# Gate/up and down of a SwiGLU layer by seven block products instead of eight

## The chip, the cores and the metric

One core of one Trainium2 chip runs the whole program, a hybrid decoder layer in float32. The metric is device time in microseconds (us), the median of several runs. The engines are TensorE (matmuls and transposes; PE in the rows, its weight loads PEld), VectorE (DVE), ScalarE (ACT), GpSimd (POOL) and SyncE (SP, which here only issues DMAs).

## What the kernel computes

The layer has a token-mixing part (four parallel mixers, gated and merged, then an output projection) and a channel-mixing part, SwiGLU. The change is in the second:

```python
h2 = rmsnorm(x, norm2_g)                      # x: 1024 tokens x 1024 features
g_ff, up_ff = jnp.split(h2 @ w_gate_up, 2, axis=-1)   # 2816 columns each
return x + (jax.nn.silu(g_ff) * up_ff) @ w_down       # then a last rmsnorm
```

## The kernel before

Every operand of a large product is held as hi + lo, two float32r values that sum to the float32 one (`split`, L126 to L128: ScalarE casts hi, VectorE subtracts to get lo), and a product is three matmuls into the same PSUM bank (`mm3`, L119 to L124). A matmul has a 128x128 stationary operand and a moving one of 128x512. Weights come from DRAM in pieces of 128 x 1024 (512 KB) by SP's queue and are split when they land (`load_w`, L111).

The 1024 tokens are two halves of 512 (HT). Tokens of half 0 are normalised and transposed while the merge of half 1 runs (the list `later`, L688 and L738); those of half 1 are written to DRAM (`x2d`), read back and normalised inside the first four blocks of gate/up (`norm2`, L747): ScalarE squares, VectorE scales the rows, TensorE turns eight pieces of 128 into two PSUM banks, `split` takes them out. The result `h2[half]` holds features on partitions, 8 pieces of 128 features by 512 tokens.

Gate/up: for each half, for each of NF = 22 blocks of 128 hidden columns, `group` (L174) makes the gate product and the up product, 8 pieces x 3 matmuls each. ScalarE takes Silu of the gate, VectorE multiplies by up, and the result is split into `ff`, which stays in SBUF (11 tiles, each two blocks). Down: `tok_out` (L647), for each half and each 512 output columns, runs over 11 pairs of hidden blocks and 4 token tiles, with `ff` as the stationary operand and the split weight as the moving one, into four PSUM banks; `evict_f` (L797) adds the residual, sums the squares for the last norm, and `store_f` scales and stores. So each half's weights of gate/up and down are loaded and split again, 88 and 44 pieces.

The order on each engine is made by the framework's scheduler: it simulates the program by a table of costs and issues what is ready, the earlier traced first; tiles of a pool tag share a fixed number of buffers, and an instruction that needs a buffer waits for its last readers. Each engine then runs its queue strictly in that order, SP's DMA issues and GpSimd's too. `in_order` (L130) fixes what is traced inside it to the traced order. PSUM has eight banks of 128x512 float32: two "mm", three "z", two "tr", one "o".

Of the kernel before, what the change touches and what calls it, by code (L numbers as in the profile page):

```python
# [46 lines left out]
def tile_hybrid_trunk(  # L47
# [19 lines left out]
    wp = ctx.enter_context(tc.tile_pool(name="wp", bufs=2))  # L67
    hp = ctx.enter_context(tc.tile_pool(name="hp", bufs=2))
    sp = ctx.enter_context(tc.tile_pool(name="sp", bufs=4))
    ps = ctx.enter_context(tc.tile_pool(name="ps", bufs=1, space=bass.MemoryType.PSUM))  # L70
# [59 lines left out]
    @contextmanager  # L130
    def in_order():
        """Keeps TensorE, ScalarE and VectorE to the order traced."""
        names = [(nc.tensor, "matmul"), (nc.tensor, "transpose"), (nc.scalar, "copy"), (nc.scalar, "activation"),
                 (nc.vector, "tensor_sub"), (nc.vector, "tensor_add"), (nc.vector, "tensor_mul"),
                 (nc.vector, "scalar_tensor_tensor"), (nc.vector, "tensor_scalar")]
# [44 lines left out]
    x2d = [dp.tile([P, D], F32, name=f"x2d{t}") for t in range(8)]  # L180

    # =============================== token mixers ===============================
# [3 lines left out]
    class Fill:  # L186
        """Projection work that is traced in between the steps of a mixer, to keep TensorE fed."""
# [140 lines left out]
    def scores(st, j, c, mask):  # L328
        """Units of at most 512 keys of the raw scores of query tile c, masked on its own block."""
# [43 lines left out]
    def attend(st, p, rows, br, per_step):  # L373
# [11 lines left out]
        def turned(pq, s0):  # L385
            """The weights of two key tiles, key-major, hi and lo."""
# [259 lines left out]
    # =============================== merge and output projection ===============================  # L646
    def tok_out(nkp, act, src, evict, last=False):  # L647
        """Token-major product of feature-major activations with a weight, 512 columns at a time."""
        for ch in range(2):
            acc = [psum("z", f"acc{i}") for i in range(3)] + [psum("o", "acc3")]  # L650
            todo = [(kp, t) for kp in range(nkp) for t in range(4)]
            if last and ch:
                # the token tiles end one after the other
                k0, k1 = nkp - 2, nkp - 1
                todo[-8:] = [(k0, 0), (k0, 1), (k1, 0), (k1, 1), (k0, 2), (k1, 2), (k0, 3), (k1, 3)]
# [10 lines left out]
            with in_order() if last and ch else nullcontext():  # L666
                for t in range(4):
                    evict(t, ch, acc[t])
# [5 lines left out]
    for half in range(2):  # L674
# [57 lines left out]
        def evict_o(t, ch, acc, half=half, x2=x2, hh=hh):  # L732
            c = slice(ch * 512, (ch + 1) * 512)
            nc.vector.tensor_add(x2[t][:, c], acc, x2[t][:, c])
            if ch == 1:
                nc.sync.dma_start(x2d[4 * half + t], x2[t])
                if half == 0:
                    later.append(lambda: norm_T(x2[t], gp.tile([P, D], F32, tag="yr", name="xn2", bufs=1),  # L738
                                                g2, hh, t * P))
# [5 lines left out]
    fp = ctx.enter_context(tc.tile_pool(name="fp", bufs=2, reuse_waits="tile"))  # L745

    def norm2(t):  # L747
        r = fp.tile([P, D], F32, tag="xr", name="x2r", bufs=4)
        nc.sync.dma_start(r, x2d[4 + t])
        norm_T(r, fp.tile([P, D], F32, tag="xr", name="xn2", bufs=4), g2, h2[1], t * P)  # L750

    for half in range(2):
        ff = []
        for f in range(NF):
            wg = load_w(wgu[2 * f])
            og = psum("mm", "mmf")
            group(og, wg, h2[half])
            wu = load_w(wgu[2 * f + 1])
            ou = psum("mm", "mmf")
            group(ou, wu, h2[half])  # L760
            sl = fp.tile([P, HT], F32, name="sl", bufs=2)
            nc.scalar.activation(sl, og, AF.Silu)
            nc.vector.tensor_mul(sl, ou, sl)  # L763
            if f % 2 == 0:
                ff.append(fp.tile([P, 2, 2, HT], F32R, tag="ff", name="fft", bufs=11))
            split(ff[-1][:, f % 2, 0, :], ff[-1][:, f % 2, 1, :], sl)
            if half == 0 and f == 0:
                g2 = load_g(fp, norm2_g, "gf", 1)
            if half == 0 and f < 4:
                norm2(f)  # L770
            if later:
                later.pop(0)()

        xr, ssf = [], []
        for t in range(4):
            r = fp.tile([P, D], F32, tag="xr", name="xr", bufs=4)
            nc.sync.dma_start(r, x2d[4 * half + t])
            xr.append(r)
            ssf.append(sp.tile([P, 2], F32, tag="ssf", name="ssf"))
        if half == 0:  # L780
            gf = load_g(fp, final_g, "gf", 1)
        lo_, hi_ = slice(0, 512), slice(512, 1024)

        def rstd_f(t, ssf=ssf):
# [94 lines left out]
```

## Time and profile before

| | |
|---|---|
| median of 3 runs | 1767.07 us (1766.25 to 1767.4) |
| profiled execution, span from first to last instruction | 1765.0 us (its own time outside the span is not listed) |
| TensorE busy | 1737.9 us, 98% |
| VectorE busy | 817.4 us, 46% |
| ScalarE busy | 606.8 us, 34% |
| DMA | 171.22 MB, 97 GB/s on average |

Busy time is the union of an engine's instructions; matmuls overlap, so the mean of one is longer than the distance from one start to the next. A group's line gives line number, engine, operation, output and inputs, shape, count, then busy time and mean, then the engine's idle time just before and what released it.

### The profile page before, as it was taken

To read this page: it belongs to the slowest core of one execution; us is meant where nothing else is said; L and a number is where in the kernel's file an instruction comes from. 1 tells how busy PE (TensorE), PEld (TensorE's weight loads), DVE (VectorE), ACT (ScalarE), POOL (GpSimd) and SP (SyncE) were. 2 spreads that over 40 slices of the span, in tenths; PEclk is the share of its full clock that TensorE was granted. 3 is DMA by queue.
4 is the path that set the end of the run, shared out by engine and by line. 5 is a ranking of instruction groups with operands and counts; after the bars stand their busy time and mean duration, and the time that the engine had idled before them with its cause. 6 is when DMAs were issued, how large, how long until landed. Compare 5 with 4: busy or idle time off the path is not lost.

```text
span 1765.0 us, 19954 instructions
## 1 busy us (share of the span) xinstructions
PE 1737.9 (98%) x7973; PEld 1396.9 (79%) x7973; DVE 817.4 (46%) x1168; ACT 606.8 (34%) x975; POOL 47.3 (3%) x108
## 2 busy tenths in 40 slices
PE   7999999999999999999999999999999999999998
PEld 7778777777788888888888888888888888888886
DVE  5676667787733435443434453333323333333232
ACT  5433455655432222243222242222212322222222
POOL 1011000010000000000000000000000000000000
PEclk9999999999999999999999999999999999999999
DMA  4311111101152223343223363222222522222222
GB/s 174 108 54 51 51 32 32 31 20 32 33 166 95 96 96 126 109 163 115 96 96 105 128 233 119 96 93 92 92 96 95 191 94 96 96 96 96 96 95 96
DMA packets 52620, 171.22 MB, mean 97 GB/s; under 512 B 6160, under 2 KB 9264, under 8 KB 52528
## 3 DMA queue, kind: packets, MB, share of 16 engines
q1 hardware_dynamic: 51952, 167.85, 28.3%
q10 hardware_dynamic: 576, 2.10, 0.4%
q8 instruction: 63, 1.03, 0.2%
q14 instruction: 29, 0.24, 0.0%
HBM read 156.27 MB, written 13.65 MB: 96 GB/s over the span
## 4 chain that ended last, share of the span: by engine, by line
PE 89%; DVE 4%; issue 1%; ACT 1%; POOL 0%; POOLq 0%; DVEq 0%; ACTq 0%
PE mmf L124 9%; PE mmf L123 9%; PE mmf L122 9%; PE mmg L124 7%; PE mmg L123 7%; PE mmg L122 7%; PE acc L124 6%; PE acc L122 6%; PE acc L123 6%; PE mm L122 3%; PE mm L124 3%; PE mm L123 3%; PE o L399 2%; PE pr L123 2%; PE pr L122 2%; PE pr L124 2%
## 5 line engine op out<-in xcount | busy, mean ns | idle before, releaser
L128 DVE TENSOR_TENSOR wlo<-wraw,whi 128x1024 fp32r<-128x1024 f32 x250 | 306.0, 1224 | 602.3 <-ACT whi L127 595.7
L127 ACT CAST whi<-wraw 128x1024 fp32r<-128x1024 f32 x250 | 262.1, 1048 | 865.4 <-PE mmf L123 317.7
L124 PE MATMUL mmf<-g0h,wlo 128*128 128x512 f32 x352 | 139.2, 396 | 0.0
L124 PE MATMUL mmf<-g1h,wlo 128*128 128x512 f32 x352 | 139.2, 395 | 0.0
L123 PE MATMUL mmf<-g1l,whi 128*128 128x512 f32 x352 | 138.7, 394 | 0.0
L123 PE MATMUL mmf<-g0l,whi 128*128 128x512 f32 x352 | 138.7, 394 | 0.0
L122 PE MATMUL mmf<-g0h,whi 128*128 128x512 f32 x352 | 138.5, 393 | 0.0
L124 PE MATMUL acc<-whi,fft 128*128 128x512 f32 x352 | 138.4, 393 | 0.0
L122 PE MATMUL acc<-whi,fft 128*128 128x512 f32 x352 | 138.3, 393 | 0.0
L122 PE MATMUL mmf<-g1h,whi 128*128 128x512 f32 x352 | 138.2, 393 | 0.0
L123 PE MATMUL acc<-wlo,fft 128*128 128x512 f32 x352 | 137.4, 390 | 0.0
L124 PE MATMUL mmg<-h1h,wlo 128*128 128x512 f32 x256 | 101.4, 396 | 0.1
L124 PE MATMUL mmg<-h0h,wlo 128*128 128x512 f32 x256 | 101.3, 396 | 0.0
L123 PE MATMUL mmg<-h0l,whi 128*128 128x512 f32 x256 | 100.9, 394 | 0.0
L123 PE MATMUL mmg<-h1l,whi 128*128 128x512 f32 x256 | 100.8, 394 | 0.0
L122 PE MATMUL mmg<-h1h,whi 128*128 128x512 f32 x256 | 100.8, 394 | 0.0
L122 PE MATMUL mmg<-h0h,whi 128*128 128x512 f32 x256 | 100.4, 392 | 0.0
L763 DVE TENSOR_TENSOR sl<-mmf,sl 128x512 f32<-128x512 f32 x44 | 30.4, 691 | 150.1 <-PE mmf L124 150.1
L122 PEld LDWEIGHTS mmf<-g1h,whi 128*128 128x128 f32 x352 | 66.6, 189 | 15.3
L122 PEld LDWEIGHTS mmf<-g0h,whi 128*128 128x128 f32 x352 | 66.6, 189 | 15.1
L123 PEld LDWEIGHTS mmf<-g1l,whi 128*128 128x128 f32 x352 | 66.1, 188 | 15.5
L123 PEld LDWEIGHTS mmf<-g0l,whi 128*128 128x128 f32 x352 | 66.1, 188 | 15.3
(245 smaller groups left out, 3187.3 us busy)
## 6 DMA issues: line engine op xcount, KB each, us to landing
wraw<-in_wgu_dram SPq DMA_DIRECT2D x88, 512.0 KB, 3.2
wraw<-in_wgate_dram SPq DMA_DIRECT2D x64, 512.0 KB, 3.2
wraw<-in_wd_dram SPq DMA_DIRECT2D x44, 512.0 KB, 3.3
wraw<-in_wmix_dram SPq DMA_DIRECT2D x22, 512.0 KB, 3.3
wraw<-in_wbr_dram SPq DMA_DIRECT2D x16, 512.0 KB, 3.2
wraw<-in_wo_dram SPq DMA_DIRECT2D x16, 512.0 KB, 3.3
xt<-in_x_dram SPq DMA_DIRECT2D x8, 512.0 KB, 9.5
yr<-ydr SPq DMA_DIRECT2D x8, 512.0 KB, 4.4
```

The lines of the kernel that those rows point to most:

```text
L122: nc.tensor.matmul(o, ah, bh, start=start, stop=False)
L123: nc.tensor.matmul(o, ah, bl, start=False, stop=False)
L124: nc.tensor.matmul(o, al, bh, start=False, stop=stop)
L127: nc.scalar.copy(hi, v)
L128: nc.vector.tensor_sub(lo, v, hi.bitcast(F32))
L399: nc.tensor.matmul(o, vv[:, s0 + s, j, :], pt[:, i, s * 256:(s + 1) * 256], start=s0 + s + i == 0, stop=s0 + s + i == ns)
L763: nc.vector.tensor_mul(sl, ou, sl)
```

## The change

The products of gate/up and of down are seen as 2x2 blocks and made by Strassen's scheme in Winograd's form: 7 block products instead of 8, with sums of blocks ahead of and behind them.

Gate/up. The left factor's blocks are gate and up weights (rows) by features 0 to 511 and 512 to 1023 (columns), for one hidden block g of 128 at a time: a11, a12, a21, a22. The right factor's blocks are the two feature halves by the two token halves. `four` makes the four sums of one factor in VectorE, the second from the first and the fourth from the second: of the weights in `blocks_w`, of the tokens in `norm2`, there still token-major, from the normalised tokens of half 0 (kept in DRAM, `xnd`, by a new DMA in `norm_T`) and of half 1. Each token tile of half 1 then has five pieces of 512 features to turn and split: h22, t1 to t4, for 2 tr banks. A product (`prod`) has 4 pieces x 3 matmuls into one of six banks. Products 1 and 2 need tokens of half 0 alone: for g = 0 to 9 they run first (`early`), with the norm of half 1 traced between them and TensorE kept to the traced order, and product 1 and the Silu of gate half 0 go to DRAM (`stash`). Then `rest` runs for g = 0 to 21: the products left, their sums out of PSUM by VectorE, Silu, multiplies.

Down. After each second block, `down_a` makes the four sums of two result blocks and stores all seven left operands in DRAM (`ffd`), and `down_b` loads the down weights, makes their four sums and stores them (`wdd`); both by GpSimd's queue. Then a second stage makes seven products one after the other (`product`), each over 11 hidden pairs and 4 token tiles into four of eight banks; each of its operands (128x512, 256 KB) is loaded from DRAM and split (`operand`). The sums out of PSUM are made by VectorE and, from SBUF, by GpSimd (16 adds of 128x512); the residual, the norm and the stores follow as output blocks become complete, the last product's four token tiles one after the other.

SBUF pools are closed and opened anew: the weight pool and the PSUM pool end after the output projection; gate/up has its own (t2 to t4; ten tiles "x4" of 128x1024 for raw weights, sums, stash, results and norm; six "x2" tiles; four split weight pairs and a fifth of half the size), and down has its own where h2, t2 to t4 and x4 were. The mixers and the layout of the inputs stay as they were.

```diff
-    def norm_T(xt, xn, g, h, c0):
+    def norm_T(xt, xn, g, h, c0, keep):
         ss = norm_stat(xt, xn)
         nc.vector.scalar_tensor_tensor(xn, xt, ss, g, op0=ALU.mult, op1=ALU.mult)
+        nc.gpsimd.dma_start(keep, xn)
         norm_turn(xn, h, c0)
...
+    pq = pqs.enter_context(tc.tile_pool(name="pq", bufs=1, space=bass.MemoryType.PSUM, reuse_waits="tile"))
+    fp = p3.enter_context(tc.tile_pool(name="fp", bufs=2, reuse_waits="tile"))
+    EARLY = 10
...
+    h11 = [v[:, 0:4] for v in h2[0]]
+    h21 = [v[:, 4:8] for v in h2[0]]
+    h22 = [v[:, 0:4] for v in h2[1]]
+    t1 = [v[:, 4:8] for v in h2[1]]
+    t2, t3, t4 = ([fp.tile([P, 4, HT], F32R, name=f"t{i}{v}", bufs=1) for v in "hl"] for i in (2, 3, 4))
+    stash = [dp.tile([P, D], F32, name=f"stash{g}") for g in range(EARLY)]
+    ffd = [dp.tile([P, 7, HT], F32, name=f"ffd{j}") for j in range(NF // 2)]
+    wdd = [dp.tile([P, 7, HT], F32, name=f"wdd{j}") for j in range(NF // 2)]
+    def tile4(name):
+        return fp.tile([P, 1024], F32, tag="x4", name=name, bufs=10)
...
+    def four(s, x11, x12, x21, x22, first):
+        if first:
+            tt(s[0], x21, x22, op=add)
+            tt(s[1], s[0], x11, op=sub)
+            tt(s[2], x11, x21, op=sub)
+            tt(s[3], x12, s[1], op=sub)
...
     def norm2(t):
...
+        s = halves(tile4("tok")) + halves(tile4("tok"))
+        four(s, a0, b0, a1, b1, False)
+        yield
+        for v, to in zip([b1] + s, (h22, t1, t2, t3, t4)):
+            tr = pq.tile([P, 512], F32, tag="tr", name="trn", bufs=2).rearrange("p (k t) -> p k t", k=4)
+            for k in range(4):
+                nc.tensor.transpose(tr[:, k, :], v[:, k * P:(k + 1) * P], identf)
+            split(to[0][:, :, c], to[1][:, :, c], tr)
+    def prod(w, h):
+        o = pq.tile([P, HT], F32, tag="pp", name="pp", bufs=6)
+        for k in range(4):
+            c = slice(k * P, (k + 1) * P)
+            mm3(o, (w[0][:, c], w[1][:, c]), (h[0][:, k, :], h[1][:, k, :]), k == 0, k == 3)
+        return o
+    def early(g):
+        w = split2(load_raw(2 * g))
+        st = tile4("st")
+        nc.scalar.copy(st[:, :512], prod(half_of(w, 0), h11))
+        tt(st[:, 512:], prod(half_of(w, 1), h21), st[:, :512], op=add)
+        nc.scalar.activation(st[:, 512:], st[:, 512:], AF.Silu)
+        nc.gpsimd.dma_start(stash[g], st)
+    def blocks_w(g):
+        r0, r1 = load_raw(2 * g), load_raw(2 * g + 1)
+        a11, a12, a21, a22 = r0[:, :512], r0[:, 512:], r1[:, :512], r1[:, 512:]
+        s23, s14 = tile4("s23"), tile4("s14")
...
+        four(s, a11, a12, a21, a22, True)
...
+    def rest(g, w):
+        if g < EARLY:
+            st = tile4("st")
+            nc.sync.dma_start(st, stash[g])
+            p1, sl = st[:, :512], st[:, 512:]
+        else:
+            p1, sl = tile2("p1"), tile2("sl")
+            nc.scalar.copy(p1, prod(w[1], h11))
+            tt(sl, prod(w[2], h21), p1, op=add)
+            nc.scalar.activation(sl, sl, AF.Silu)
+        u2, u3 = tile2("u2"), tile2("u3")
+        tt(u2, prod(w[6], t2), p1, op=add)
+        tt(u3, prod(w[7], t3), u2, op=add)
+        p5 = prod(w[5], t1)
+        tt(u2, p5, u2, op=add)
+        up = tile2("up")
+        tt(up, p5, u3, op=add)
+        tt(u3, prod(w[4], t4), u3, op=add)
+        tt(u2, prod(w[3], h22), u2, op=add)
+        nc.scalar.activation(u2, u2, AF.Silu)
+        ff = tile4("ff").rearrange("p (t c) -> p t c", t=2)
+        nc.vector.tensor_mul(ff[:, 0], u3, sl)
+        nc.vector.tensor_mul(ff[:, 1], up, u2)
+        return ff
+    def down_a(j, e, o):
+        q = nc.gpsimd
+        s = [tile4("fs") for _ in range(2)]
+        four(halves(s[0]) + halves(s[1]), e[:, 0], o[:, 0], e[:, 1], o[:, 1], True)
+        q.dma_start(ffd[j][:, 0], e[:, 0])
+        q.dma_start(ffd[j][:, 1], o[:, 0])
+        q.dma_start(ffd[j][:, 2], o[:, 1])
+        for i in range(2):
+            q.dma_start(ffd[j][:, 3 + 2 * i:5 + 2 * i], s[i].rearrange("p (t c) -> p t c", t=2))
...
+    with in_order([(nc.tensor, "matmul"), (nc.tensor, "transpose")]):
+        for g in range(EARLY):
+            early(g)
+            if g % 2 == 0 and g // 2 + 1 < 4:
+                next(turns[g // 2 + 1])
+            if g % 2 == 1 and g // 2 < 4:
+                next(turns[g // 2], None)
+    nxt = blocks_w(0)
+    for g in range(NF):
+        w = nxt
+        if g + 1 < NF:
+            nxt = blocks_w(g + 1)
+        ff = rest(g, w)
+        if g % 2 == 0:
+            down_b(g // 2)
+            last = ff
+        else:
+            down_a(g // 2, last, ff)
...
+    def operand(src):
+        r = dn.tile([P, HT], F32, tag="dr", name="dr", bufs=8)
+        nc.sync.dma_start(r, src)
+        h, l = (dn.tile([P, HT], F32R, tag=f"d{v}", name=f"d{v}", bufs=10) for v in "hl")
+        split(h, l, r)
+        return h, l
+    def product(na, nb, stagger=0):
+        acc = [pd.tile([P, HT], F32, tag="acc", name="acc", bufs=8) for _ in range(4)]
...
+                ops[j] = operand(ffd[j][:, na]), operand(wd_of(nb, j))
+            (ah, al), b = ops[j]
+            tl = slice(t * P, (t + 1) * P)
+            mm3(acc[t], (ah[:, tl], al[:, tl]), b, j == 0, j == NJ - 1)
```


## Rows read from the trace of the kernel before

**Rows 1.** The page: busy us (share, count) by engine; granted clock in 40 slices.
```profile
PE 1737.9 (98%) x7973; PEld 1396.9 (79%) x7973; DVE 817.4 (46%) x1168; ACT 606.8 (34%) x975; POOL 47.3 (3%) x108
...
PEclk9999999999999999999999999999999999999999
```

**Rows 2.** The page: the chain that ended last, share by engine.
```profile
PE 89%; DVE 4%; issue 1%; ACT 1%; POOL 0%; POOLq 0%; DVEq 0%; ACTq 0%
```

**Rows 3.** Busy us (count) by engine in five stretches; then clock, DMA share, GB/s.
```profile
1021.20:1269.90 248.70, 248.25 (x1089) 201.95 (x1088) 91.72 (x103) 79.22 (x104) 2.19 (x4) 1.00 0.36 123
1269.90:1391.60 121.70, 121.70 (x530) 99.11 (x529) 35.29 (x40) 28.24 (x36) 0.55 (x1) 1.00 0.29 95
1391.60:1636.40 244.80, 244.80 (x1058) 198.93 (x1057) 84.75 (x95) 72.79 (x95) 1.65 (x3) 1.00 0.33 112
1636.40:1758.10 121.70, 121.70 (x529) 98.90 (x528) 35.86 (x43) 28.81 (x38) 1.10 (x2) 1.00 0.27 90
1758.10:1765.00 6.90, 0.20 (x1) 0.00 (x0) 2.26 (x4) 2.06 (x4) 1.10 (x2) 0.88 0.47 181
```

**Rows 4.** Groups of instructions by shape: count, busy us, mean ns, idle before.
```profile
L124 PE MATMUL mmf<-g0h,wlo 128*128 128x512 f32 x352 | 139.2, 396 | 0.0
...
L122 PE MATMUL mmf<-g1h,whi 128*128 128x512 f32 x352 | 138.2, 393 | 0.0
...
L124 PE MATMUL acc<-whi,fft 128*128 128x512 f32 x352 | 138.4, 393 | 0.0
```

**Rows 5.** The chain in order of time from 1000 us: start, us, what.
```profile
1045.31 0.87 PE trn L161 x8
```

**Rows 6.** Order of time around the first norm of half 1: start us, us, instruction.
```profile
1034.24 1.28 DVE L166 SCALAR_TENSOR_TENSOR xn<-x2r,ss,g_sb 128x1024 f32<-128x1024 f32 x1 [0.73 <-POOL ss L148]
...
1035.68 1.06 PE L161 MATMUL trn<-identf,xn 128*128 128x128 f32 x8 [0.45 <-DVE xn L166]
...
1036.95 1.05 ACT L127 CAST g1h<-trn 128x512 fp32r<-128x512 f32 x2
...
1037.55 1.29 DVE L128 TENSOR_TENSOR g1l<-trn,g1h 128x512 fp32r<-128x512 f32 x2 [0.22 <-ACT g1h L127]
```

**Rows 7.** Order of time on VectorE in the merge.
```profile
854.85 0.69 DVE L707 TENSOR_TENSOR pr_sb<-pr,sig 128x512 f32<-128x512 f32 x1
855.58 0.69 DVE L711 TENSOR_TENSOR pr_sb<-pr_sb 128x512 f32<-128x512 f32 x1
856.19 1.22 DVE L128 TENSOR_TENSOR wlo<-wraw,whi 128x1024 fp32r<-128x1024 f32 x1
857.32 0.69 DVE L128 TENSOR_TENSOR mgt<-pr_sb,mgt 128x512 fp32r<-128x512 f32 x1
```

**Rows 8.** DMA from 1021 to 1040 us: rate; issues with us to landing.
```profile
DMA packets 1587, 5.78 MB, mean 304 GB/s; under 512 B 180, under 2 KB 180, under 8 KB 1586
...
wraw<-in_wgu_dram SPq DMA_DIRECT2D x3, 512.0 KB, 5.3
```

**Rows 9.** One tile's instructions on GpSimd: ns min/median/max.
```profile
L560 POOL TENSOR_TENSOR yc<-xst,head_sb x8: 607/612/1476, 82.7 to 165.0; 128x256 f32<-128x256 f32 x8
```

**Rows 10.** The page: DMA queues that carry data; its most frequent issue.
```profile
q1 hardware_dynamic: 51952, 167.85, 28.3%
q10 hardware_dynamic: 576, 2.10, 0.4%
...
wraw<-in_wgu_dram SPq DMA_DIRECT2D x88, 512.0 KB, 3.2
```

**Rows 11.** Order of time on TensorE near the start.
```profile
12.64 0.42 PE L138 MATMUL mmz<-whi,h0h 128*128 128x260 f32 x1
12.86 0.42 PE L138 MATMUL mmz<-wlo,h0h 128*128 128x260 f32 x1
...
16.40 0.28 PE L138 MATMUL mmz<-whi,h0h 128*128 128x260 f32 x1
16.52 0.29 PE L138 MATMUL mmz<-wlo,h0h 128*128 128x260 f32 x1
```

More of the change, by code (lines that the diff above doesn't have):

```diff
@@ L19 @@
-from contextlib import ExitStack, contextmanager, nullcontext
+from contextlib import ExitStack, contextmanager
 import concourse.bass as bass
@@ L180, in tile_hybrid_trunk @@
     x2d = [dp.tile([P, D], F32, name=f"x2d{t}") for t in range(8)]
+    xnd = [dp.tile([P, D], F32, name=f"xnd{t}") for t in range(4)]
     p1 = ExitStack()
@@ L665, in tok_out @@
                         kp + k2 == 0, kp == nkp - 1 and k2 == 1)
-            with in_order() if last and ch else nullcontext():
-                for t in range(4):
-                    evict(t, ch, acc[t])
+            for t in range(4):
+                evict(t, ch, acc[t])
     p2 = ExitStack()
@@ new lines, in pair_w, with load_raw, split2, half_of @@
+    def pair_w(n=1024):
+        return [fp.tile([P, n], F32R, tag=f"w{v}{n}", name=f"w{v}", bufs=4 if n == 1024 else 1) for v in "hl"]
+    def load_raw(f):
+        raw = tile4("raw")
+        nc.sync.dma_start(raw, wgu[f])
+        return raw
+    def split2(v):
+        w = pair_w(v.shape[-1])
+        split(*w, v)
+        return w
+    def half_of(w, i):
+        return [v[:, i * 512:(i + 1) * 512] for v in w]
+    def halves(v):
+        return [v[:, :512], v[:, 512:]]
+    def prod(w, h):
[4 more added lines that the diff above has]
+        return o
@@ new lines, in tile_hybrid_trunk @@
+    g2 = tile4("g2")
+    nc.scalar.dma_start(g2, norm2_g.partition_broadcast(P))
+    turns = [norm2(4 + i) for i in range(4)]
+    next(turns[0])
+    with in_order([(nc.tensor, "matmul"), (nc.tensor, "transpose")]):
[6 more added lines that the diff above has]
+    nxt = blocks_w(0)
+    last = None
+    for g in range(NF):
[6 more added lines that the diff above has]
+            last = ff
+        else:
+            down_a(g // 2, last, ff)
@@ new lines, in tile_hybrid_trunk, with rstd_f @@
+    p3.close()
+    p0.close()
+    pqs.close()
+    dn = ctx.enter_context(tc.tile_pool(name="dn", bufs=2, reuse_waits="tile"))
+    xr = []
+    for t in range(8):
+        r = dn.tile([P, D], F32, tag="xr", name="xr", bufs=8)
+        nc.scalar.dma_start(r, x2d[t])
+        xr.append(r)
+    gf = load_g(dn, final_g, "gf", 1)
+    ssf = [sp.tile([P, 2], F32, tag="ssf", name="ssf", bufs=8) for _ in range(8)]
+    lo_, hi_ = slice(0, 512), slice(512, 1024)
+    def rstd_f(t):
+        nc.vector.scalar_tensor_tensor(ssf[t][:, 1:2], ssf[t][:, 1:2], 1.0 / D, ssf[t][:, 0:1],
+                                       op0=ALU.mult, op1=ALU.add)
+        nc.gpsimd.tensor_tensor(ssf[t][:, 1:2], ssf[t][:, 1:2], nhalf[:, 0:1], op=ALU.pow)
@@ new lines, in first_half @@
+    def first_half(t, c):
+        square(t, c, 0)
+        nc.vector.tensor_scalar(ssf[t][:, 0:1], ssf[t][:, 0:1], 1.0 / D, EPS, op0=ALU.mult, op1=ALU.add)
+        nc.vector.tensor_mul(xr[t][:, c], xr[t][:, c], gf[:, c])
+    pd = ctx.enter_context(tc.tile_pool(name="pd", bufs=1, space=bass.MemoryType.PSUM, reuse_waits="tile"))
+    NJ = NF // 2
+    def operand(src):
[4 more added lines that the diff above has]
+        return h, l
@@ new lines, in keep @@
+    def keep(name):
+        return [dn.tile([P, HT], F32, tag=name, name=name, bufs=4) for _ in range(4)]
+    p1, u2, u3 = keep("p1"), keep("u2"), keep("u3")
+    pool_add = lambda o, v: nc.gpsimd.tensor_tensor(o, o, v, op=add)
+    X = product(0, 0)
+    for t in range(4):
+        nc.scalar.copy(p1[t], X[t])
+        pool_add(xr[t][:, lo_], p1[t])
+    X = product(1, 1)
+    for t in range(4):
+        tt(xr[t][:, lo_], X[t], xr[t][:, lo_], op=add)
+        first_half(t, lo_)
+    X = product(4, 4)
@@ new lines, in tile_hybrid_trunk @@
+    for t in range(4):
+        tt(u2[t], X[t], p1[t], op=add)
+    X = product(5, 5)
+    for t in range(4):
+        tt(u3[t], X[t], u2[t], op=add)
+        pool_add(xr[4 + t][:, lo_], u3[t])
+        pool_add(xr[4 + t][:, hi_], u3[t])
+    X = product(3, 3)
+    for t in range(4):
+        tt(u2[t], X[t], u2[t], op=add)
+        tt(xr[4 + t][:, hi_], X[t], xr[4 + t][:, hi_], op=add)
+        pool_add(xr[t][:, hi_], u2[t])
+        first_half(4 + t, hi_)
+    X = product(2, 6)
+    for t in range(4):
+        tt(xr[4 + t][:, lo_], X[t], xr[4 + t][:, lo_], op=add)
+        square(4 + t, lo_, 1)
+        rstd_f(4 + t)
+        store_f(4 + t, hi_)
@@ L816 @@
+    X = product(6, 2, stagger=3)
+    with in_order():
+        for t in range(4):
+            tt(xr[t][:, hi_], X[t], xr[t][:, hi_], op=add)
+            square(t, hi_, 1)
+            for fn, i in {0: (), 1: ((rstd_f, 0), (store_f, 0), (rstd_f, 1), (store_f, 1)), 2: ((rstd_f, 2),),
+                          3: ((store_f, 2), (rstd_f, 3), (store_f, 3))}[t]:
+                fn(*((i,) if fn is rstd_f else (i, lo_)))
 _ARGS = ["x", "wmix", "wzdt", "wgate", "wbr", "wo", "wgu", "wd", "norm1_g", "norm2_g", "final_g",
```

142 lines of the change are left out of this document (73 added, 69 removed).

## The prediction

> **What bounds the kernel now.** I read the busy times first, then the chain of waits, then the stretches of the feed-forward part, then the gaps inside them. TensorE is busy 1737.9 us of a span of 1765.0 us, VectorE 817.4 and ScalarE 606.8 [rows 1]; the chain that ended last is 89% TensorE [rows 2]. In the four stretches that the change replaces (gate/up of half 0, down of half 0, gate/up of half 1, down of half 1) TensorE has no idle time worth naming: 248.7, 121.7, 244.8 and 121.7 us, all but 0.45 us busy, while VectorE works 29 to 37% of them [rows 3]. So a matmul taken out there is worth its pace, and VectorE has room. The pace is not the 393 to 396 ns that a matmul lasts in the groups [rows 4], because successive ones overlap: 1056 matmuls of gate/up (three groups of 352) fill 244.8 us, 0.2318 us each, and 528 of down fill 121.7 us, 0.2305 us each [rows 3, 4]. Whoever prices the removed work by the duration is out by 70%.
>
> **TensorE's sum.** Gate/up has 6 groups of 352, that is 2112 matmuls; after, 22 blocks x 7 products x 4 pieces x 3 = 1848, so 264 fewer: 264 x 0.2318 = 61.2 us. Down has 3 groups of 352, 1056; after, 7 x 11 x 4 x 3 = 924, so 132 fewer: 30.4 us. Added are transposes: each of 4 token tiles of half 1 turns five pieces of 512 features where it turned two, 80 transposes for 32. Eight of them take 0.87 us [rows 5], so 48 more cost 5.2 us. Net on TensorE: -86.4 us. All the rest of the sum is time in which TensorE would wait.
>
> **First tokens of half 1.** The ten early blocks (products 1 and 2 of g = 0 to 9, 24 matmuls each) need only half 0, and their order with the transposes is fixed. TensorE comes to the first tile's transposes after two blocks, 48 x 0.2318 = 11.1 us after 1021.2, at 1032.3. Before, that tile's scaled rows are ready at 1034.24 + 1.28 = 1035.5, by a load through DRAM that starts when the tile is stored; TensorE waited for it then too, only less [rows 6]. I take 3 us; 0 if the loads land sooner, 6 if the four new differences (0.7 us each) come ahead too.
>
> **Transposes.** Five pieces share two PSUM banks. Before, two pieces each had a bank: started at 1035.68, cast at 1036.95, the second subtraction ended at 1038.84 [rows 6], so a bank is held 2.5 to 3.2 us. Pieces 3 and 5 wait a turn each: 5.4 us or, with ScalarE free at once (two casts 1.05), 3.4, against 2.2 unhindered: 1.2 to 3.2 us for each of 4 tiles, 5 to 13 us. I take 8.
>
> **Second pass, g = 0 to 9.** TensorE: five products, 60 matmuls, 13.9 us a block. VectorE: four weight sums, six product sums, two multiplies, and per block half of two further sets of four (down's operands, down's weights): 16 operations on 128x512; then one subtraction of 1024 and three of 512. Successive VectorE operations of 512 start 0.61 us apart when independent, 0.73 when one reads the other's result; one of 1024 takes 1.13 [rows 7]. That makes 16 x 0.61 + 1.13 + 3 x 0.61 = 12.7 us to 16 x 0.73 + 1.13 + 3 x 0.73 = 15.0 us, on either side of 13.9. VectorE stops being spare here; six PSUM banks and weights one block ahead soften it. 0 to 1.1 us a block by this, and 1.3 more if each of the six sums waits 0.22 us for another engine, as a row shows [rows 6]: 0 to 24 us in all; I take 0.8 a block, 8 us. ScalarE's casts of 512 take 0.53 us each in a pair [rows 6], some 3 us a block: spare.
>
> **g = 10 to 21.** 84 matmuls, 19.5 us; VectorE 17 operations and 2 x 1.13 + 3 x 0.61: 14.5 to 16.9 us. I take 3 us in all (0 to 12, 1 a block).
>
> **The step into down.** PSUM, the h tiles and x4 change hands; down's split pieces lie where t2 to t4 were, free only after the last products that read them, so the first operand is cast and subtracted in the last 2.8 us of gate/up (12 x 0.2318) or just after it. 2 us, between 0 and 8.
>
> **Down.** A product has 132 matmuls, 30.4 us. It splits 22 operands: VectorE 22 x 0.61 plus four to eight sums, 17 to 19 us; ScalarE 22 x 0.53 = 11.6. It loads 22 x 256 KB, 5.77 MB, 190 GB/s; the second pass before it moves some 3.4 MB in 13.9 us, 245 GB/s. The crowded stretch before reached 304 GB/s, a 512 KB load landing in 5.3 us [rows 8]. Down is hidden: 0, at most 5. GpSimd's 16 adds of 512 lie beside matmuls: at 256 elements one took 612 ns, at most 1476 [rows 9], so twice that is 20 to 47 us of 214. The last chain after the last matmul (6.9 us [rows 3]) keeps its steps.
>
> **GpSimd's stores.** In the trace the data go through the two queues q1 and q10, those of SP and ACT [rows 10], so none of the some 90 stores now issued by GpSimd is shown. Bounds: landing between the 3.2 us of most loads [rows 10] and 5.3 [rows 8]; I take 5.3, for the queues will be full. They hold x4 tiles, not TensorE, unless the tiles run out (below).
>
> **Clock.** TensorE's first matmuls of 260 columns, with no work on it before them, start 0.22 us apart; from 16.40 on the same ones start 0.12 apart: half pace, then full, the levels of 1.2 and 2.4 GHz [rows 11]. The clock column reads 9 or more in all 40 slices [rows 1], even in that first one, so the pace itself has to be watched: through the wait of 0.45 us before the first transposes [rows 6] gate/up of half 0 kept it, 248.7 us against 244.8 plus 3.5 for 32 transposes [rows 3, 5]. The Trainium skill ("TensorE: Matmul & The Clock Gate", section "A second HAM failure mode: psum-queue depth-cycling") says that short idles between groups of matmuls which cycle through PSUM banks can make the clock swing between its two levels. The second pass would be such a stretch by that rule; it makes rival (d) and no term here.
>
> **Sum.** Waits 3 + 8 + 8 + 3 + 2 = 24 us. Span 1765.0 - 86.4 + 24 = 1702.6. The median of the runs, 1767.07, lies 2.07 above the profiled span: 1704.7.
>
> **Rivals.**
> (a) All waits hide and only 5 us at the transposes stay: 1765.0 - 86.4 + 5 + 2.1 = 1685.7, at the best 1681. For it: six banks are 16.6 us of slack between TensorE and VectorE (6 x 12 x 0.2318), and VectorE is idle two thirds of these stretches now. Against: the transposes' order is fixed.
> (b) VectorE becomes the bound in the second pass and every term is at its upper end: 6 + 13 + 24 + 12 + 8 + 5 = 68 us, 1748.7. For it: 15.0 above 13.9. Against: that takes every operation as dependent.
> (c) Slower: the weights stop being one block ahead. Raw weights, sums, spilled results and their stores share ten x4 tiles; if stores hold them so long that the raw pair of block g + 1 is issued only when block g's last products run, each block exposes a load of 5.3 us [rows 8]: 22 x 5.3 = 117 us, 1765.0 - 86.4 + 5 + 3 + 117 + 2.1 = 1805.7. It decides from 86.4 / 22 = 3.9 us a block. For it: SP waits in order behind whichever load has no tile yet, and no row shows how long a store by GpSimd holds its tile. Against: an estimate of tile time per block, in us: two raw tiles 9 each (a load, then the sums), two sum tiles 7 each, the stash 17 (from its load to the block's last multiply), the result 19 (it waits for its pair), half of down's four raw and sum tiles and two spilled ones 28; together 96 against 139 available (10 x 13.9).
> (d) Also slower: the waits of the second pass bring half pace. Sixty matmuls at twice 0.2318 add 13.9 us a block, 139 us over ten: 1704.7 + 139 = 1843.7. For it: the half pace near the start [rows 11]. Against: a wait of 0.45 us did not bring it [rows 6], and the waits forecast are of that size. The rule of the Trainium skill cited above is this rival's.
>
> **Chances.** Forecast (1690 to 1725) 0.50, (a) 0.19, (b) and what lies between it and the forecast (1725 to 1763) 0.18, no change 0.02, (c) 0.08, (d) 0.03. The range 1683 to 1748 leaves out the slower cases, the best of (a) and the worst of (b). About 0.2% is what a measurement of this kernel can tell from no change. Faster 0.87, same 0.02, slower 0.11.
>
> **What would show it.** TensorE's matmul count down by 396 at the same pace of 0.231; idle before the transposes released by ScalarE or VectorE, about 11 us in all; in the second pass TensorE idle under a microsecond a block with VectorE above 90% busy, then about 75 to 85% from g = 10; down's products each 30.4 us. It is wrong if TensorE's idle sits on weights (subtractions fed by late loads, rival c), if VectorE is busy all the time and TensorE's stretch of a block is over 15 us (b), or if matmuls of 512 start more than 0.3 us apart with nothing to wait for (d).

## The result, and the profile after

The changed kernel takes 1784.41 us (median of 4 runs, 1783.36 to 1785.43) against 1767.24 us (1766.25 to 1768.02, 4 runs): ratio 1.0097, 95% interval 1.0083 to 1.0111. It is slower by 17 us; 1704.7 us was forecast, with a range that ended at 1748.

The page of the changed kernel: busy time of two engines, the granted clock in 40 slices, and the queue that was not there before.

```profile
PE 1669.1 (94%) x7625; PEld 1338.2 (75%) x7625; DVE 1066.1 (60%) x1626; ACT 638.7 (36%) x1101; POOL 122.0 (7%) x215
...
PEclk9999999999999999999999968899999999899999
...
q0 software_dynamic: 10992, 39.07, 5.4%
```

TensorE works 69 us less than in [rows 1] (348 fewer matrix instructions: 396 matmuls out, 48 transposes in), and yet the span is 18.6 us longer. Four slices of the clock read 6, 8, 8 and 8 where none was below 9: three over the early blocks, one at the step into down. So the saving was there, and waits, with a slower clock behind them, took it; the stretches say where. Columns as in [rows 3]: the early blocks, the second pass to g = 9 and on, the step into down, its first 6 us, down, the tail.

```profile
1027.00:1172.80 145.80, 84.12 (x321) 63.42 (x320) 51.28 (x70) 39.12 (x61) 7.74 (x14) 0.78 0.37 129
1172.80:1312.00 139.20, 139.15 (x605) 114.28 (x606) 125.87 (x190) 34.59 (x53) 16.69 (x31) 0.99 0.66 234
1312.00:1541.00 229.00, 227.82 (x1004) 188.05 (x1002) 179.86 (x266) 63.46 (x93) 23.18 (x43) 1.00 0.44 154
1541.00:1559.00 18.00, 0.00 (x0) 0.00 (x0) 4.31 (x7) 1.78 (x4) 1.62 (x3) 0.60 0.96 357
1559.00:1565.00 6.00, 5.95 (x13) 4.39 (x14) 4.41 (x8) 3.11 (x6) 0.00 (x0) 0.50 1.03 416
1565.00:1771.60 206.60, 206.60 (x912) 170.86 (x911) 130.98 (x201) 99.19 (x184) 28.45 (x22) 1.00 0.62 195
1771.60:1783.60 12.00, 0.22 (x1) 0.00 (x0) 2.86 (x6) 2.78 (x6) 1.10 (x2) 0.72 0.39 149
```

The second pass, where most of the doubt had been, is full: TensorE idles 0.05 and 1.2 us in 368. The large losses stand at its two ends. Forecast beside measured, in us of the profiled span:

| stretch | forecast, by its own terms | measured | more |
|---|---|---|---|
| to the end of the output projection | 1021.2 | 1027.0 | +5.8 |
| early blocks and transposes | 240 x 0.2318 + 80 x 0.87/8 + 3 + 8 = 75.3 | 145.8 | +70.5 |
| second pass | 1608 x 0.2318 + 8 + 3 = 383.7 | 368.2 | -15.5 |
| step into down | 2 | 18.0 | +16.0 |
| down | 924 x 0.2305 = 213.0 | 212.6 | -0.4 |
| tail | 6.9 | 12.0 | +5.1 |

The first row of difference that matters is the early pass. What TensorE waited for in the whole changed kernel (total us, times, longest; `pp` at L145 is the early blocks, `trn` at L145 the transposes beside them, `pp` at L129 the second pass), and then what SP's queue waited for from 1020 to 1180 us (L810 loads raw weights):

```profile
PE pp L145 <- ACT wh L134: 37.5, 4, 9.6
PE acc L129 <- ACT dh L134: 18.2, 1, 18.2
...
PE pp L145 <- DVE wl L135: 9.4, 3, 6.0
PE trn L145 <- DVE t2l L135: 5.7, 4, 1.4
PE trn L145 <- DVE g1l L135: 5.3, 8, 1.0
...
PE pp L129 <- ACT wh L134: 3.7, 1, 3.7
```

```profile
SPq L810 <- DMA stash<-st: 36.5, 5, 15.4
...
SPq L810 <- DVE xn L794: 16.9, 1, 16.9
SPq L810 <- DVE wl L135: 13.1, 3, 7.0
```

TensorE waits for split weights (wh, wl), and SP cannot issue their loads, for an x4 tile becomes free only when a stash has been stored or a token row has been read. The stretch adds up: TensorE is idle 61.7 us of it, 50.6 for split weights (37.5, 9.4 and 3.7) and 11.0 at the transposes (5.7 and 5.3), and it is busy 84.1 us for work priced at 64.3. One turn of that wheel, in the chain of waits of the changed kernel (start us, us, what):

```profile
1084.36 0.64 ACT st L837
...
1085.29 2.85 DMA stash<-st
...
1088.20 3.36 DMA raw<-in_wgu_dram
...
1091.59 1.05 ACT wh L134
...
1093.94 6.98 PE pp L145 x22
```

Activation, store, load, cast, matmul, one after the other; and the 22 matmuls then take 6.98 us, 0.32 each, where the pace is 0.23: the granted clock is 0.78 over the stretch, so the waits are followed by slower matmuls, 19.8 us in all (84.1 less 64.3).

### The profile page after: what moved, and what is told of

The parts are those of the page before. It is cut to its first block, busy times and chain, and to the rows that moved or that the text cites. A ratio compares the mean times of both kernels' runs of the same rounds, so it can differ in the third digit from the quotient of the medians.

```text
span 1783.6 us, 20511 instructions
## 1 busy us (share of the span) xinstructions
PE 1669.1 (94%) x7625; PEld 1338.2 (75%) x7625; DVE 1066.1 (60%) x1626; ACT 638.7 (36%) x1101; POOL 122.0 (7%) x215
## 4 chain that ended last, share of the span: by engine, by line
PE 77%; DVE 9%; DMA 3%; ACT 3%; issue 2%; POOL 0%; POOLq 0%; ACTq 0%; DVEq 0%; SPq 0%
PE mmg L130 6%; PE mmg L131 6%; PE mmg L129 6%; PE acc L129 6%; PE acc L130 6%; PE acc L131 6%; PE pp L129 5%; PE pp L131 5%; PE pp L130 5%; PE pp L145 4%; PE mm L129 3%; PE mm L131 3%; PE mm L130 3%; PE o L408 2%; PE pr L131 2%
## 5 line engine op out<-in xcount | busy, mean ns | idle before, releaser
L135 DVE TENSOR_TENSOR wlo<-wraw,whi 128x1024 fp32r<-128x1024 f32 x118 | 144.3, 1223 | 272.8 <-ACT whi L134 269.9
L134 ACT CAST whi<-wraw 128x1024 fp32r<-128x1024 f32 x118 | 123.6, 1048 | 352.7 <-PE mmg L130 199.8
L135 DVE TENSOR_TENSOR dl<-dr,dh 128x512 fp32r<-128x512 f32 x154 | 109.0, 755 | 80.0 <-ACT dh L134 80.0
L129 PE MATMUL acc<-dh 128*128 128x512 f32 x308 | 121.2, 393 | 18.2 <-ACT dh L134 18.2
L134 ACT CAST dh<-dr 128x512 fp32r<-128x512 f32 x154 | 88.7, 619 | 111.2 <-PE acc L130 81.1
L130 PE MATMUL acc<-dl,dh 128*128 128x512 f32 x308 | 121.0, 393 | 0.0
L131 PE MATMUL acc<-dh,dl 128*128 128x512 f32 x308 | 120.8, 392 | 0.0
L129 PE MATMUL mmg<-h1h,whi 128*128 128x512 f32 x256 | 101.7, 397 | 0.8 <-ACT whi L134 0.8
L129 PE MATMUL mmg<-h0h,whi 128*128 128x512 f32 x256 | 101.2, 395 | 0.0
L129 PEld LDWEIGHTS acc<-dh 128*128 128x128 f32 x308 | 58.5, 190 | 30.7 <-ACT dh L134 18.7
L129 PE MATMUL mm<-h0h,whi 128*128 128x512 f32 x176 | 74.4, 423 | 0.0
L145 PE MATMUL pp<-g0h,wh 128*128 128x512 f32 x80 | 38.3, 479 | 37.5 <-ACT wh L134 37.5
L129 PE MATMUL mm<-h1h,whi 128*128 128x512 f32 x176 | 73.2, 416 | 0.0
L131 PE MATMUL mm<-h0h,wlo 128*128 128x512 f32 x176 | 70.5, 401 | 0.5 <-DVE wlo L135 0.5
L130 PE MATMUL mm<-h0l,whi 128*128 128x512 f32 x176 | 70.8, 402 | 0.0
```

Of the source, the lines that this page charges most:

```text
L129: nc.tensor.matmul(o, ah, bh, start=start, stop=False)
L130: nc.tensor.matmul(o, ah, bl, start=False, stop=False)
L131: nc.tensor.matmul(o, al, bh, start=False, stop=stop)
L134: nc.scalar.copy(hi, v)
L135: nc.vector.tensor_sub(lo, v, hi.bitcast(F32))
```

## The experiments

All are compared with the kernel before (1766.5 to 1766.8 us beside them); the changed kernel is at 1784.41. A ring is the fixed number of buffers that the tiles of one tag share.

**The early pass.** e1 takes the raw weights out of the crowded ring:

```diff
-        w = split2(load_raw(2 * g))
+        w = pair_w()
+        for i in range(2):
+            raw = tile2("raw2")
+            nc.sync.dma_start(raw, wgu[2 * g][:, i * 512:(i + 1) * 512])
+            split(*half_of(w, i), raw)
```

> The changed kernel with one thing different: the raw weights of the ten early blocks go into two tiles of 512 columns (the tag x2, which the early pass leaves unused) instead of one of the ten tiles x4. Theory (tiles run out: a block's raw weights wait until an x4 tile that holds a stash or a norm's token row is free, so they are loaded when they are already needed): the stretch of 145 us between the output projection and the second pass shrinks to 90 to 110 us, the time to about 1735 us (1730 to 1750), and the wait of the raw loads for the stash's store is gone from SP's waits. Rival 1 (the pass is slow because VectorE and ScalarE have the turned tokens and their splits to do, with the transposes in the matmuls' order): the stretch stays within 10 us of 145 and the time above 1775 us. Rival 2 (the loads are late because SP's own queue stands behind the stores of the token rows, not for want of tiles): the first block's weights come no earlier, 10 to 15 us are won, about 1770 us.

Measured 1743.06 us (1742.13 to 1743.63), ratio 0.9867 (0.9852 to 0.9881). The early stretch went from 145.8 to 101.7 us, and the wait of these loads for the stash is gone:

```profile
1027.00:1128.70 101.70, 75.30 (x322) 59.97 (x320) 50.31 (x79) 40.67 (x71) 7.73 (x14) 0.88 0.53 187
```

The theory's size holds on the wide side (101.7 in 90 to 110), rivals 1 and 2 do not. The edit also halves the pieces in which these weights are loaded and split, which no run separates from the other ring; that the ring held the loads up is what SP's waits above show. One edit turns the slower kernel into a faster one. What is left was asked of e6, which traces the second norm behind the ten blocks (the lines that it has beside those of e1):

```diff
-    next(turns[0])
...
-            if g % 2 == 0 and g // 2 + 1 < 4:
-                next(turns[g // 2 + 1])
-            if g % 2 == 1 and g // 2 < 4:
-                next(turns[g // 2], None)
+        for t in turns:
+            next(t)
+            next(t, None)
```

> The kernel of e1_early_raw_x2 with the second norm's four token tiles traced behind the ten early blocks, not in between. It left 101 us for the early stretch. Theory (what is left there is weights' subtractions behind the norm's items on VectorE and transposes that wait in the matmuls' fixed order): the stretch falls to 80 to 90 us and the time to 1725 to 1735 us. Rival (the start is DMA-bound and the rest is half clock after it): within 5 us of 1743 us. A third outcome, slower than 1743 us, would say that the turned tokens are then late for the second pass.

Measured 1747.21 us (1746.57 to 1749.5). By the time alone both the rival (within 5 us of 1743) and the third outcome hold; the trace speaks for the third, and this run explains the most. Its chain of waits, and a stretch of it in the norm:

```profile
1033.69 57.67 PE pp L145 x240
1091.44 0.70 DVE st L840
1092.71 1.14 ACT xn L159 x2
...
1102.79 1.16 ACT xn L159 x2
...
1123.06 1.16 ACT xn L159 x2
```

```profile
1100.00:1120.00 20.00, 10.38 (x40) 7.23 (x40) 14.45 (x22) 7.75 (x14) 1.10 (x2) 0.50 0.33 98
```

The ten blocks alone run without a break, 0.240 us a matmul where the forecast had 0.2318. The norm alone is a chain of 10.1 us for each token tile, 43 us for four, at a granted clock of 0.50. So each should hide the other if neither stands in the other's fixed order. f0, also built on e1, lays them out so: from the third block on, one group of four transposes behind each product (`step()`), a fifth behind every second block, and a tile's arithmetic traced ahead of them.

```diff
             split(to[0][:, :, c], to[1][:, :, c], tr)
+            yield
...
         nc.scalar.copy(st[:, :512], prod(half_of(w, 0), h11))
+        step()
         tt(st[:, 512:], prod(half_of(w, 1), h21), st[:, :512], op=add)
+        step()
...
+            step = (lambda: next(turns[g // 2 - 1], None)) if g > 1 else (lambda: None)
+            early(g, step)
+            if g % 2:
+                step()
+            elif g < 8:
+                next(turns[g // 2])
```

> The kernel of e1_early_raw_x2 with the second norm's work between the early blocks laid out anew: a token tile's five groups of four transposes stand one behind each early product from the third block on, two blocks to a tile, and the VectorE half of that tile is traced two blocks ahead. e6 showed 240 matmuls in 57.7 us without the norm between them, and then 43 us of the norm alone in a row; e1 101 us for both mixed. Theory (the ten blocks and the norm can hide each other, about 58 us of matmuls and 8.7 us of transposes, behind 6 to 7 us of start): the stretch takes 70 to 80 us and the time 1715 to 1728 us. Rival (VectorE, in its fixed order, still holds the weights' subtractions behind the norm's items): 1735 us or more.

Measured 1718.97 us (1717.76 to 1721.36), ratio 0.973 (0.9716 to 0.9745), in the theory's range; the stretch is 82 us (expected 70 to 80). TensorE is idle 12.0 us of it: 5.5 for the first weights, 2.1 for a token row, 4.4 for the first weights of the second pass.

```profile
1027.00:1109.00 82.00, 69.99 (x326) 56.90 (x325) 51.10 (x81) 40.30 (x71) 7.75 (x14) 0.93 0.67 237
```

```profile
PE pp L145 <- ACT wh L134: 5.5, 1, 5.5
...
PE pp L129 <- ACT wh L134: 4.4, 1, 4.4
PE trn L145 <- DVE xn L794: 2.1, 1, 2.1
```

**The step into down.** In the changed kernel ScalarE issues eight reloads and a gain before it may cast the first operands; TensorE waits. ScalarE's and TensorE's instructions in order of time:

```profile
1541.70 13.80 ACTq L937 DMA_DIRECT2D xr<-x2d  x8
...
1557.85 4.26 ACT L134 CAST dh<-dr 128x512 fp32r<-128x512 f32 x8 [15.60 <-DMA xr<-x2d]
```

```profile
1559.04 0.80 PE L129 MATMUL acc<-dh 128*128 128x512 f32 x1 [18.24 <-ACT dh L134]
```

e2 moves these issues behind the first product and to SP:

```diff
-        nc.scalar.dma_start(r, x2d[t])
...
     X = product(0, 0)
+    for t in range(8):
+        nc.sync.dma_start(xr[t], x2d[t])
+    nc.sync.dma_start(gf, final_g.partition_broadcast(P))
```

> The changed kernel with one thing different: the eight reloads of the residual rows (4.2 MB) and the final norm's gain are issued behind the first down product, on SP's queue, not ahead of it on ScalarE's. Theory (the 18.2 us without a matmul in the step into down are ScalarE's casts of the first operands, queued behind the issue of those reloads, and the operands' loads beside them): the gap shrinks to 4 to 9 us, the 6 us at half pace behind it go too, and the time comes to 1768 to 1774 us. Rival (the gap is the down operands' own loads, which can start only when the old pools are closed, through memory written just before): the gap stays at 14 us or more, and the time above 1780 us.

Measured 1781.78 us (1778.81 to 1783.78): 2.6 us won where the theory expected 10 to 16. The cast was early now, and the next wait took its place (VectorE, then TensorE, of e2):

```profile
1554.57 3.70 DVE L135 TENSOR_TENSOR dl<-dr,dh 128x512 fp32r<-128x512 f32 x6 [6.13 <-DMA ffd<-fs]
```

```profile
1547.81 0.80 PE L129 MATMUL acc<-dh 128*128 128x512 f32 x1 [4.80 <-ACT dh L134]
...
1555.31 0.80 PE L130 MATMUL acc<-dl,dh 128*128 128x512 f32 x1 [6.71 <-DVE dl L135]
```

The second subtraction waits for a store of the pool just closed: in the compiled program the second tile of the ring dl lies at byte 139264, inside the x4 tile (from 137216) whose last content that store reads. Both the theory and the rival were incomplete; the cause had two layers. e5 removes both, by opening dn's rings over tokens that the last block reads first (lines cut to the order of the tags):

```diff
+    first = [ring("dr", F32, 8)]
+    p1, u2 = keep("p1"), keep("u2")
+    first.append(ring("dh", F32R, 10))
+    u3 = keep("u3")
+    gf = dn.tile([P, D], F32, tag="gf", name="g_sb", bufs=1)
+    first.append(ring("dl", F32R, 10))
```

> The changed kernel with the residual rows' reload behind the first down product (as in e2_xr_late) and with the tiles of the pool dn laid in another order, so that the ring of loaded operands and their two splits lie over the tokens h11, h21, t2 and t3, which the last block of the second pass reads first, not over t4 and over the x4 tiles whose last store is read out by a DMA. Theory (the gap in the step into down has two covers that each hide it: the casts queue behind the reloads on ScalarE, and the second subtraction waits on VectorE until the last 512 KB store has left the tile under it): the gap falls from 18.2 to under 4 us, the half pace behind it goes, and the time to 1755 to 1766 us. Rival (the operands are late because SP issues their loads only after the last block's): the gap stays over 8 us and the time over 1772 us.

Measured 1773.73 us (1772.32 to 1773.8): 10.7 us won, less than the theory's 18 to 29. TensorE waits 2.53 us, does one matmul and waits 3.05 us: 5.6 us, between the two bounds, and the half pace behind it stayed. TensorE's order of time and then e5's chain: what is left is the last block's own arithmetic, with down's subtraction queued behind four sums on VectorE.

```profile
1542.00 0.50 PE L129 MATMUL acc<-dh 128*128 128x512 f32 x1 [2.53 <-ACT dh L134]
1545.55 0.79 PE L130 MATMUL acc<-dl,dh 128*128 128x512 f32 x1 [3.05 <-DVE dl L135]
```

```profile
1540.29 0.64 ACT u L878
1540.95 0.70 DVE ff L881
1541.68 0.69 DVE fs L775
...
1544.82 0.69 DVE dl L135
```

**The pace.** Where nothing interrupts it, in the changed second pass and in its down stage a matmul follows the last in 0.226 us, in the kernel before in 0.2318 and 0.2305 [rows 3, 4]; in the stages that both share, the changed kernel is the slower one. Three stretches of the changed kernel, all TensorE:

```profile
1180.00:1300.00 120.00, 120.00 (x531) 99.00 (x530) 107.75 (x166) 27.38 (x41) 15.09 (x28) 1.00 0.67 236
1320.00:1520.00 200.00, 200.00 (x884) 165.65 (x883) 162.13 (x238) 59.19 (x85) 20.11 (x38) 1.00 0.47 165
1570.00:1760.00 190.00, 190.00 (x840) 157.34 (x839) 124.16 (x189) 92.65 (x172) 27.35 (x20) 1.00 0.64 201
```

Five runs on the kernel before tell why. e3 opens the pools sp, hp and wp in the changed kernel's order and edits nothing else:

> The kernel before with one thing different: its three small pools are opened in the changed kernel's order (sp, hp, wp), which moves the addresses of the weight and token tiles and nothing else. In the changed kernel the merge and the output projection, which it shares with the kernel before, run at 0.2324 us from matmul to matmul against 0.2311. Theory (the pace of a matmul whose operands are resident hangs on where its tiles lie): the pace of this stage is 0.2320 or more, and the time 5 to 12 us above the kernel before. Rival (the pace there comes from other traffic of the changed kernel): pace and time as before within 0.1%.

Measured 1772.43 us (1772.16 to 1772.7), ratio 1.0034 (1.0021 to 1.0046): 5.9 us for an order of pools, in the theory's range. This is not the +5.8 of the table's first row, though it is as large: e3's first matmul of gate/up starts at 1022.9 us against 1021.4 in the kernel before, so only 1.5 us are lost by then. What else the first row holds was not separated; with a distance of 1088 (f1, below) it is gone. pw1088 sets the constant PW to 1088:

> The kernel before with one number different: the padded width of its weight tiles is 1088 columns for 1040, so each half of a weight pair starts at another distance. In the changed kernel's second pass and in its down stage matmuls follow each other in 0.229 and 0.226 us, in the kernel before in 0.2318 and 0.2305. Theory (placement: those tiles are 1024 columns wide and aligned, the old ones 1040): pace in gate/up falls towards 0.227, and the time by 5 to 13 us. Rival (the pace of the changed kernel comes of other things: fewer transfers beside it, or the order of the weights): no change within 0.2%.

Measured 1752.85 us (1752.56 to 1755.32), ratio 0.9926 (0.9911 to 0.994): 13.7 us won, a little over the range. e7 puts 128 bytes between weights and tokens, e8 moves the weights by 128 and leaves the tokens, e9 has both off by 128:

```diff
+    pad1 = ctx.enter_context(tc.tile_pool(name="pad1", bufs=1))
+    nc.gpsimd.memset(pad1.tile([P, 32], F32, name="pad1_t"), 0.0)
...
-        raw = wp.tile([P, PW], F32, name="wraw")
+        raw = wp.tile([P, 1088], F32, name="wraw")
...
-        hi = wp.tile([P, PW], F32R, name="whi")
-        lo = wp.tile([P, PW], F32R, name="wlo")
+        hi = wp.tile([P, 1088], F32R, name="whi")
+        lo = wp.tile([P, 1088], F32R, name="wlo")
```

This is e7 (the pad stands between wp and hp). e8 and e9 leave raw at 1040, which moves the split weights by 128; e8 has a pad of 96 for 32, e9 none.

> The kernel before with weight tiles at a distance of 1088 columns (weights at multiples of 256 bytes, as in pw1088) and 128 bytes of padding between weights and tokens, so that the token tiles lie 128 bytes past a multiple of 512, which in pw1088 they hit. Theory A (the pace hangs on where the weights lie): as pw1088, 1750 to 1756 us. Theory B (it hangs on where the moving tokens lie): as the kernel before, 1763 to 1770 us. Between: both count.

> The counterpart: token tiles exactly where they lie in pw1088 (a multiple of 512 bytes), weight tiles 128 or 384 bytes past such a multiple. Theory A (weights' place): as the kernel before, 1763 to 1770 us. Theory B (tokens' place): as pw1088, 1750 to 1756 us.

> The kernel before with weight tiles at 128 or 384 bytes past a multiple of 512 (as in e8_weights_128) and token tiles at 128 past it (as in e7_tokens_128): both are off by the same 128 bytes. If what counts is each operand's own place: as e7 and e8, 1763 to 1767 us. If what counts is the one's place against the other's: as pw1088, 1751 to 1756 us.

Measured 1763.76 (1762.77 to 1764.24), 1764.28 (1763.62 to 1764.8) and 1752.71 us (1752.19 to 1753.18). e7 alone spoke for the tokens, e8 alone for the weights; e9 shows that, at steps of 128, neither's own place counts but their difference. Groups of one gate/up and one down matmul (count, busy us, mean ns) of pw1088, then of e7 and, alike in every figure, e8, then of e9:

```profile
L122 PE MATMUL mmf<-g1h,whi 128*128 128x512 f32 x352 | 137.0, 389 | 0.0
...
L123 PE MATMUL acc<-wlo,fft 128*128 128x512 f32 x352 | 138.9, 395 | 0.0
```

```profile
L124 PE MATMUL mmf<-g1h,whi 128*128 128x512 f32 x352 | 139.0, 395 | 0.0
...
L125 PE MATMUL acc<-wlo,fft 128*128 128x512 f32 x352 | 137.0, 389 | 0.0
```

```profile
L122 PE MATMUL mmf<-g1h,whi 128*128 128x512 f32 x352 | 136.9, 389 | 0.0
...
L123 PE MATMUL acc<-wlo,fft 128*128 128x512 f32 x352 | 138.9, 395 | 0.0
```

The first bytes modulo 256 of the split weights, the tokens and fft in the compiled programs are 0/0/128, 0/128/0, 128/0/128 and 128/128/0. In all eight cases a group has 389 ns where its two operands agree and 395 where they differ by 128; the other seven groups of the feed-forward part in each run lie within 1 ns of this. That moves down the other way from gate/up in each run, which fits the 2 to 3 us that e7 and e8 still won. The kernel before also has differences of 64 and 192, whose pace no run separates.

**The end, and all together.** In the changed kernel the span ends 7.1 us after the last store is issued, in the kernel before 3.1. e10 issues one early load of the kernel before on GpSimd's queue (`nc.gpsimd.dma_start(chan_sb, chan)`):

> The kernel before with one small load at its start (the channels' constants) issued on GpSimd's DMA queue, which the kernel before doesn't use and the changed kernel does. From the last matmul to the end of the span the kernel before takes 6.9 us, the changed one 11.8 us with the same chain of work. Theory (a program that uses this queue ends later): the tail is 11 to 12 us and the time 1770 to 1773 us. Rival (the tail is longer because of what is in flight in the changed kernel): tail and time as before, 1766 to 1768 us.

Measured 1767.12 us (1766.5 to 1767.34), ratio 1.0002 (0.9992 to 1.0011): one early load is not it. f1 puts f0, e5's step and a distance of 1088 together:

> f0_early_interleaved with the step into down of e5_down_rings and the weight tiles of the stages before at a distance of 1088 columns for 1040, so that weights lie at multiples of 256 bytes and tokens at multiples of 512 everywhere. If the three parts add up: f0's time less 10.7 us (e5 against the changed kernel) less 7 to 10 us (1536 gate matmuls and 2 x 192 of the output projection and the mixers' projections, at about 0.005 us each), 1695 to 1712 us. If the parts share their gain or the placement does nothing here: f0's time less 10 us or so, 1708 to 1720 us.

Measured 1696.76 us (1696.33 to 1699.3), ratio 0.9606 (0.9591 to 0.962): 22.2 us below f0, in the range of parts that add up: 10.7 for the step as e5 has it leave 11.5 for the placement by difference, and the output projection does end at 1014.9 us where it ended at 1027.0. f2 takes every spill off GpSimd's queue (`nc.gpsimd.dma_start` and `q = nc.gpsimd` become ScalarE's):

> f1_all with all spills (normed tokens, stash, operands of down) issued on ScalarE's queue, so that GpSimd's DMA queue is not used at all. In the changed kernel and in f1_all the span ends 5 us after the last store has landed, in the kernel before about 1 us after it, and one early load on GpSimd's queue did not lengthen the kernel before. Theory (the program's end waits for something that a much used GpSimd queue leaves behind): the end falls from about 7 us after the last store's issue to about 3 us, and the time by 4 us if the spills cost ScalarE nothing, 1691 to 1694 us. Rival (the end is long for another reason): the tail stays at 7 us, and the time is 1696 us or more, more where the issues hold up ScalarE's casts.

Measured 1690.5 us (1688.58 to 1691.63), ratio 0.957 (0.9554 to 0.9586). The last issue of SP in the kernel before (span 1765.0), the changed kernel (1783.6) and f2 (1686.9):

```profile
1761.87 0.38 SPq L795 DMA_DIRECT2D out_dram<-xr  x1
```

```profile
1776.49 0.38 SPq L955 DMA_DIRECT2D out_dram<-xr  x1
```

```profile
1683.69 0.38 SPq L968 DMA_DIRECT2D out_dram<-xr  x1
```

That leaves 3.1, 7.1 and 3.2 us (7.1 in f1): with some 90 stores on that queue the program ends 4 us later, with none it does not. Why one early load costs nothing stays open, and so do the other 2 us of the 6.3 by which f2 is below f1.

## Why the prediction was wrong, step by step

- **First tokens of half 1: the step that failed.** It priced the early blocks as matmuls at 0.2318 us plus 3 us for the first transposes, and the loads of their weights at nothing. Where a load can land was asked for the norm, whose rows came in time, not for the blocks' weights. They shared ten x4 tiles with stash, rows and token sums, and a block's matmuls last only 5.6 us (24 x 0.2318) there, against 13.9 in the second pass. TensorE waited 50.6 us for split weights, and at the lower clock it was busy 19.8 us longer than priced. This is rival (c)'s mechanism, in a place where it was not looked for: its estimate of 96 of 139 us of tile time was made for the second pass, where TensorE idled 0.05 us up to g = 9. Price: 7 us a block (70.5 / 10); (c)'s limit of 3.9 was for 22 blocks, for ten the same saving of 86.4 gives 8.6, so this loss takes most of the saving, and the step into down, the tail and the table's first row the rest. e1 shows 41.4 us of it to go with the ring; f0 another 24.1 with the order of norm and blocks. The 82.0 us left exceed the forecast's 75.3 by 6.7: 1.0 more of waits (12.0 for 11) and 5.7 of slower matmuls (70.0 busy for 64.3, clock 0.93).
- **Transposes.** The size was right: the changed kernel's waited 11.0 us for the subtractions that empty their two banks, three waits a tile, in the forecast's 5 to 13. The 3 us for a late first row did not come. In f0 the banks' waits are gone; one of 2.1 us for a row is left.
- **Step into down: 2 us said, 18 measured**, plus about 3 us of half pace on its first 13 matmuls. It was asked when the operands' tiles come free, but not what stands ahead of their cast on ScalarE (nine DMA issues), nor whose store still reads the memory under the ring. Both are in the diff.
- **Second pass.** Forecast 11 us of waits, measured 1.2 us (the 3.7 for its first weights are in the row above); VectorE at 90% and then 79%, as said. Its upper bounds (rival (b)) were far too wide. That six PSUM banks and weights one block ahead are what covers a VectorE at 90% was argued; no run changes either.
- **Clock, rival (d).** The rule of the Trainium skill ("TensorE: Matmul & The Clock Gate", section "A second HAM failure mode: psum-queue depth-cycling") made no price in the second pass: through 368 us of cycling banks the granted clock is 0.99 and 1.00, but these had hardly an idle to try it on; whether it has a part in the early pass, no run separates. The clock fell where TensorE had waited: 0.78 in the early pass (waits of up to 9.6 us, price 19.8 us), 0.50 behind the step (18.2 us, price 3). So half pace did cost time, but in other stretches than (d)'s. The forecast's reading of the start [rows 11] also overlooked eight transposes, from 9.57 us on, ahead of the matmuls that it says had no work before them.
- **TensorE's sum.** Right in its count, with a gift that was luck: the new tiles agree modulo 256, which at 0.226 for 0.2318 is worth 9 us in the second pass (1608 x 0.0058) and 4 us in down (924 x 0.0043), where it hides the half pace. Not foreseen, and it hid part of the loss.
- **Tail: "keeps its steps"** held for the instructions, not for the end of the program (+5.1, of which 4 by GpSimd's queue; the last 1 is not explained).

The forecast's own number, 1704.7, lies between f0 and f1, but f1 has a gain by placement that the forecast did not count and that the kernel before can have too. Against pw1088 (1752.85), f1 is 56.1 us and f2 62.4 us faster: of the 86.4 us saved on TensorE, about two thirds arrive.

## What to carry to other kernels

When a stage is split in two, count tile time for the shorter part by itself: so many tiles held for so long, against buffers times that part's shorter block (the count was not made here, so how near it would have come is not shown). At a change of pools ask of each first instruction of the new stage what is queued ahead of it on its engine and which last reader, a store above all, owns the bytes under its tile. A stall that has gone names only the layer that was on top, so one removed cause is no estimate of the gain (e2: 2.6 us of 18).

## What the runs showed of the hardware that was not expected

- A matmul of 128x128 by 128x512 (fp32r) repeats in 389 or 395 ns as recorded, 0.226 or 0.232 us from one to the next, by whether its two operands' addresses in a partition agree modulo 256 or differ by 128 (pw1088, e7, e8, e9: eight of eight groups shown). 13.7 us in 1767 for one padding constant.
- A wait on TensorE is followed by a price in pace: behind the step's 18.2 us, 13 matmuls took 5.95 us at a granted clock of 0.50, some 3 us more than at full pace; the 2.53 and 3.05 us that e5 left had matmuls 0.43 us apart behind them too.
- With some 90 DMAs on GpSimd's queue the program ended 7.1 us after its last store was issued (changed kernel, f1), with the same ones on ScalarE's 3.2 us (f2); one early load on it did not change the time (e10).
